# A hybrid decoder block on eight cores: from hand order to a list schedule, with the input projections by seven block products

## The chip, the cores and the metric

The kernel runs on the eight NeuronCores of one Trainium2 chip. Each core does one sequence of the batch; the cores share no data. The metric is the time of one execution in device microseconds, that of the slowest core. A core has five engines with their own in-order instruction queues: TensorE (PE, matmul, with its weight loads PEld), VectorE (DVE), ScalarE (ACT), GpSimd (POOL) and SyncE (SP). They wait for each other with semaphores. Matmuls write into banks of a memory called PSUM (`ps` in the traces), which ScalarE and VectorE read out. GLA is the gated linear attention of the code below.

Some executions fall into a slower state: the cores of one die, or of both, are granted a lower TensorE clock, and the run takes 2 to 16% longer.

## The reference, cut to what matters

```python
D_MODEL, BATCH, SEQ = 2048, 8, 2048      # one batch element a core
u = rmsnorm(h)
# one input projection, 12,816 columns wide, cut into ten parts
aq, ak, av, gq, gk, gv, g_lr, g_r, gate_a, gate_b = split(u @ w_in)
attn_o = swa_sink_attention(aq, ak, av, sinks)      # 32 heads, window 128, softmax with a sink
gate_logit = g_lr @ gla_gate_w2 + gla_gate_b        # rank 16
gla_o = gla(gq, gk, gv, log_sigmoid(gate_logit)/16) # 4 heads, chunks of a linear attention
gla_o = rmsnorm(gla_o) * silu(g_r)
h = h + (sigmoid(gate_a) * attn_o + sigmoid(gate_b) * gla_o) @ w_out
h = h + (silu(v2 @ w_gate) * (v2 @ w_up)) @ w_down  # v2 = rmsnorm(h), hidden 5632
out = rmsnorm(h)
```

The "mixer" below is everything from the input projection to the merged branches. The kernel treats the 2048 tokens in two halves of 1024.

## The kernel before: the parts that the change touches

The mixer's projections are plain matmuls, 16 steps of 128 along the contraction, with 512 moving columns:

```python
def proj_feat(c, units, col0, hf, m=128):
    b = nps()
    mm([(b[0:m, :], wu[units[k // 8]][:, k % 8, col0:col0 + m],
         xx[:, k, hf * 512:(hf + 1) * 512], k == 0, k == 15) for k in range(16)], ...)
```

The FFN's up projections already use seven block products in place of eight: a 2x2 block product after Strassen and Winograd, with sums of weights (`ws`) and of inputs (`xs`) made on VectorE beforehand, and partial products combined afterwards. Two column groups (`q`) alternate, so that a bank has two products' time, 3.5 us, to be read out.

The order is written by hand: generators that are woven together, and each engine runs its instructions in program order.

```python
prev = chain2(ov, a_chain(c, h, range(NT)))       # GLA chain, then attention of head h
weave(g_proj(c, h), prev, 32, 18)                 # ... woven into the projections of head h+1
```

In attention, the mask is a multiplication on VectorE, and the softmax sums are a matmul by ones over both key blocks, next to the value product:

```python
act(pt[:], banks[half][:, :], AF.Exp, scale=0.125)
vtt(p3, p3, amask[:, kb, :].unsqueeze(1).to_broadcast([128, 4, 128]), ALU.mult)
...
for b, kind in ((bd, 0), (bo, 1)):     # bd: sums by ones, bo: values; kb 1 and 0, both halves
    ... items.append((b[half * 64:half * 64 + 64, :], l_, e8["a_P%d" % (half * 2 + kb)][:], ...))
    mm(items)
```

The softmax here doesn't subtract the row's maximum and nothing guards it: scores larger than these inputs give would overflow.

## Time and profile before

| kernel before | |
|---|---|
| median of the first 3 runs | 3831.0 us (3831.0, 4110.6 in the slow state, 3801.0) |
| span of the profiled core | 3798.9 us |
| PE, DVE, ACT, POOL busy | 95%, 43%, 31%, 5% |
| mean granted clock | 0.981 |

The head of the profile page, with the busy time of each engine, and the two rows of the 40-slice timeline for PE and for its clock (each digit is tenths):

```profile
span 3798.9 us, 47609 instructions; the slowest of 8 cores (3779.1 to 3798.9 us)
PE 3593.0 (95%) x17296; PEld 1623.0 (43%) x17296; DVE 1633.8 (43%) x2661; ACT 1187.8 (31%) x2231; POOL 195.1 (5%) x354
PE   3899999998999999899889999999979999999997
PEclk9999999998999999999999999999999999999999
```

PE is busy nearly always, but "busy" hides things, because a recorded matmul lasts 0.38 us and the next one starts after 0.216 us. The price of a matmul is read from starts. The next fence has lines of three answers of the PE timeline (start, length, what, how many in a row):

```profile
138.20 1.04 PE L332 MATMUL ps<-wu_67,xnT_108 128*128 128x256 bf16 x8
139.08 1.04 PE L332 MATMUL ps<-wu_66,xnT_108 128*128 128x256 bf16 x8
...
143.63 1.89 PE L332 MATMUL ps<-wu_69,xnT_108 128*128 128x512 bf16 x8
145.36 1.89 PE L332 MATMUL ps<-wu_68,xnT_108 128*128 128x512 bf16 x8
...
606.03 1.89 PE L332 MATMUL ps<-wu_67,xnT_108 128*128 128x512 bf16 x8
607.85 0.61 PE L621 MATMUL ps<-a_q_110,kT_109 64*128 64x512 bf16 x4
608.39 1.90 PE L332 MATMUL ps<-wu_66,xnT_108 128*128 128x512 bf16 x8
```

Eight matmuls of 512 columns take 145.36 - 143.63 = 1.73 us, 0.216 us each. Eight of 256 take 0.88 us, 0.109 each. The last three lines show: the product that starts at 606.03 is through at 607.76, but the four half-array matmuls of attention (64 rows) start at 607.85; they need two times 0.216 us, until 608.28, and the next full product starts at 608.39. Going into the half-array form and out of it cost 0.09 and 0.11 us. Such a trip is called an excursion below.

PE's waits in the kernel before, from the view of waits (total us, times, longest):

```profile
PE ps L332 <- DVE xnT_108 L376: 31.9, 2, 16.7
PE ps L332 <- DVE hy_0_152 L365: 29.5, 2, 15.4
PE ps L332 <- ACT g_la L356: 25.2, 1, 25.2
PE ps L867 <- DVE fb_2_145 L365: 10.7, 1, 10.7
```

They are few and long: the start (`xnT`, `g_la`), and changes of stage (`hy`, `fb`).

### The profile page before, as it was taken

How to read it: one execution, taken by the hardware profiler on the slowest of the kernel's cores; microseconds unless marked ns; L12 is line 12 of the kernel's file. 1: busy time of each engine (PE TensorE's matmuls, PEld its weight loads, DVE VectorE, ACT ScalarE, POOL GpSimd, SP SyncE). 2: the span in 40 equal slices, each digit the busy share in tenths (PEclk: the TensorE clock that was granted, in tenths of full speed). 3: DMA queues.
4: the chain of work that ended last, by engine and by line, in shares of the span. 5: the costliest groups of instructions: out<-in, count | busy, mean ns of one | idle time of the engine just before them, and what ended most of it. 6: DMA issues, size and time to landing. Idle time of an engine off the chain costs nothing.

```text
span 3798.9 us, 47609 instructions; the slowest of 8 cores (3779.1 to 3798.9 us)
## 1 busy us (share of the span) xinstructions
PE 3593.0 (95%) x17296; PEld 1623.0 (43%) x17296; DVE 1633.8 (43%) x2661; ACT 1187.8 (31%) x2231; POOL 195.1 (5%) x354
## 2 busy tenths in 40 slices
PE   3899999998999999899889999999979999999997
PEld 1444444443444444344344444444434444444443
DVE  1224444444476621565212344444454775146623
ACT  1243535353333300222113444454533222012212
POOL 0000000000000000000000000000001000000000
PEclk9999999998999999999999999999999999999999
DMA  7344444444565688555973342425256687874474
GB/s 159 48 67 73 67 73 67 69 63 79 167 131 119 124 168 179 67 89 105 218 163 75 59 81 46 93 45 95 45 133 159 130 168 159 193 150 86 86 158 133
DMA packets 104504, 416.93 MB, mean 110 GB/s; under 512 B 12752, under 2 KB 13904, under 8 KB 69712
## 3 DMA queue, kind: packets, MB, share of 16 engines
q0 software_dynamic: 36432, 260.19, 40.7%
q1 hardware_dynamic: 67840, 153.68, 13.4%
q8 instruction: 141, 2.31, 0.3%
q14 instruction: 91, 0.75, 0.1%
HBM read 612.14 MB, written 60.82 MB: 177 GB/s over the span
## 4 chain that ended last, share of the span: by engine, by line
PE 87%; DMA 5%; DVE 4%; ACT 1%; issue 1%; SPq 0%; POOL 0%; DVEq 0%; ACTq 0%; POOLq 0%
PE ps L332 59%; PE ps L867 27%; DMA xts_225<-xT 1%; DMA px_230<-xT 1%; PE ps L340 1%; PE ps L621 1%; DMA wu_68<-wffn 1%; DMA h_0_99<-x 1%; DMA xts_226<-xT 1%; DVE xnT_108 L376 1%; DMA yd<-hy_6_158 1%; ACT g_Sb L356 0%; SPq L385 0%; DMA h1d<-hy_6_158 0%; DVE mT L370 0%
## 5 line engine op out<-in xcount | busy, mean ns | idle before, releaser
L356 ACT ACTIVATE g_Sb<-g_U,dec 128x512 bf16<-128x512 f32 x112 | 77.2, 722 | 151.6 <-DVE g_U L376 149.1
L370 DVE TENSOR_SCALAR mT<-ps,cols_sb 128x128 bf16<-128x128 bf16 x256 | 72.6, 283 | 107.1 <-PE ps L340 85.3
L332 PE MATMUL ps<-xnT_108,wu_66 128*128 128x512 bf16 x352 | 86.4, 390 | 31.9 <-DVE xnT_108 L376 31.9
L332 PE MATMUL ps<-wu_69,xnT_108 128*128 128x512 bf16 x384 | 90.8, 379 | 0.0
L332 PE MATMUL ps<-wu_70,xnT_162 128*128 128x512 bf16 x384 | 90.8, 379 | 0.0
L356 ACT ACTIVATE a_t_96<-a_t_96 128x512 f32<-128x512 f32 x64 | 40.4, 631 | 154.9 <-DVE a_t_96 L376 154.9
L332 PE MATMUL ps<-xnT_108,wu_67 128*128 128x512 bf16 x352 | 84.4, 383 | 1.2 <-DVE g_gn_85 L376 1.2
L867 PE MATMUL ps<-v2T_114,ws_0_141 128*128 128x512 bf16 x352 | 81.2, 385 | 3.2 <-DVE ws_0_141 L365 3.2
L867 PE MATMUL ps<-v2T_168,ws_0_195 128*128 128x512 bf16 x352 | 81.0, 384 | 3.2 <-DVE ws_0_195 L365 3.2
L332 PE MATMUL ps<-xnT_162,wu_68 128*128 128x512 bf16 x352 | 83.2, 379 | 0.0
L332 PE MATMUL ps<-xnT_162,wu_67 128*128 128x512 bf16 x352 | 83.2, 379 | 0.0
L400 POOL TENSOR_TENSOR st<-st,mhalf 128x1 f32<-128x1 f32 x80 | 47.9, 599 | 631.6 <-DVE st L372 631.6
L867 PE MATMUL ps<-v2T_114,ws_1_142 128*128 128x512 bf16 x352 | 79.6, 379 | 0.0
L867 PE MATMUL ps<-v2T_168,ws_1_196 128*128 128x512 bf16 x352 | 79.6, 379 | 0.0
L362 DVE CAST g_v<-ps 128x512 bf16<-128x512 f32 x32 | 22.1, 692 | 132.3 <-PE ps L332 131.4
L332 PE MATMUL ps<-xnT_108,wu_70 128*128 128x512 bf16 x320 | 76.6, 383 | 0.0
L332 PE MATMUL ps<-wu_68,xnT_108 128*128 128x512 bf16 x320 | 75.7, 379 | 0.0
L332 PE MATMUL ps<-wu_69,xnT_162 128*128 128x512 bf16 x320 | 75.7, 379 | 0.0
L332 PE MATMUL ps<-wu_70,xnT_108 128*128 128x512 bf16 x320 | 75.7, 379 | 0.0
L332 PE MATMUL ps<-wu_66,xnT_162 128*128 128x512 bf16 x320 | 75.7, 379 | 0.0
L332 PE MATMUL ps<-xnT_162,wu_69 128*128 128x512 bf16 x320 | 75.6, 379 | 0.0
L332 PE MATMUL ps<-xnT_108,wu_68 128*128 128x512 bf16 x320 | 75.6, 379 | 0.0
(1322 smaller groups left out, 7654.7 us busy)
## 6 DMA issues: line engine op xcount, KB each, us to landing
wu_67<-wmix POOLq DMA_DIRECT2D x24, 1024.0 KB, 13.5
wu_68<-wmix POOLq DMA_DIRECT2D x24, 1024.0 KB, 13.3
wu_66<-wmix POOLq DMA_DIRECT2D x23, 1024.0 KB, 12.3
wu_69<-wmix POOLq DMA_DIRECT2D x23, 1024.0 KB, 11.4
wu_70<-wmix POOLq DMA_DIRECT2D x22, 1024.0 KB, 13.2
wu_69<-wffn POOLq DMA_DIRECT2D x19, 1024.0 KB, 13.3
wu_70<-wffn POOLq DMA_DIRECT2D x19, 1024.0 KB, 13.5
wu_66<-wffn POOLq DMA_DIRECT2D x17, 1024.0 KB, 11.6
```

The lines of the kernel that those rows point to most:

```text
L332: r = e.matmul(o_, lhsT=l_, rhs=r_, start=s0, stop=s1)
L340: r = e.transpose(out=o_, in_=i_, identity=identb[:])
L356: S.op("act", lambda e: e.activation(out=o_, in_=i_, func=func, scale=scale, **kw), outs, ins)
L362: S.op("dve", lambda e: e.tensor_copy(out=o_, in_=i_), [o_], [i_])
L370: S.op("dve", lambda e: e.tensor_scalar(out=o_, in0=a, scalar1=s1, scalar2=None, op0=op0), [o_], ins)
L376: S.op("dve", lambda e: e.scalar_tensor_tensor(out=o_, in0=a, scalar=s, in1=b, op0=op0, op1=op1), [o_], ins)
L400: S.op("pool", lambda e: e.tensor_tensor(out=r, in0=a, in1=mhalf[:, 0:1], op=ALU.pow), [r], [a, mhalf[:, 0:1]])
L621: r = e.matmul(o_, lhsT=l_, rhs=r_, start=s0, stop=s1)
L867: r = e.matmul(bank[:, :], lhsT=w[:, k, :], rhs=x[:, k, :], start=first and k == 0, stop=k == 7, skip_group_check=True)
```

## The change

The kernel is written anew. Its intent, in four parts:

1. All mixer projections by seven block products too (k and v of the first half excepted): one matmul in eight goes away, and the partial products are combined on ScalarE and VectorE, now for one column group at a time.
2. The order is computed. Every operation gets a priority tag and a modelled cost. A list schedule then simulates all engines: on each engine it takes, of the operations that can start about earliest (within 0.08 us), the one with the lowest tag, and it gives temporaries their buffers and PSUM banks on the way. The result is a fixed order per engine, with the semaphore waits that it needs.
3. The masks move to GpSimd, and the softmax sums are added over the two key blocks on VectorE before the matmul by ones.
4. The gate logits, before an fp32 matmul, become one bf16 matmul over split operands.

Also, the first norm is done by token rows and transposed, and the output and down projections use pairs of 256-column matmuls. The core of the diff (cuts marked with `...`; most of the 1181 added lines are the same work in the new form):

```diff
+    LAT = 55.0
+    MARGIN = 80.0
...
+        def release(o):
+            t = 0.0
+            for p in o.preds:
+                lat = 0.0 if p.eng == o.eng and not p.dma and not o.dma and o.eng == "pe" else self.LAT
+                t = max(t, p.end + lat)
...
+            m = min(c[0] for c in cands) + self.MARGIN
+            for c in cands:
+                if c[0] <= m:
+                    return c
...
+    def groups(gs, order=(4, 2, 1, 5, 3, 7, 6), lead=12.0, cls="b"):
...
+                if m == 4:
+                    prod(True)
+                    z["m4"] = ftile("b")
+                    acopy(z["m4"][:], b[:, :], bonus=B)
+                elif m == 2:
+                    prod(True)
+                    vtt(z["m4"][:], b[:, :], z["m4"][:], ALU.add, bonus=B)
...
-            for half in range(2):
-                pt = e8["a_P%d" % (half * 2 + kb)]
-                act(pt[:], banks[half][:, :], AF.Exp, scale=0.125)
-                p3 = pt[:, :].rearrange("p (a b) -> p a b", a=4)
-                vtt(p3, p3, amask[:, kb, :].unsqueeze(1).to_broadcast([128, 4, 128]), ALU.mult)
...
+                    act(p[:], b[:, :], AF.Exp, scale=0.125)
+                    ...
+                    S.op("pool", lambda e, ...: e.affine_select(out=real(p3), in_=real(p3), pattern=pat, ...),
+                         [p3], [p3], cost=600.0)
...
+            mm(items, cost=125.0 * len(items))          # values
+            items = []
+            for half in range(2):
+                if len(kbs) == 2:
+                    vtt(P[(1, half)][:], P[(1, half)][:], P[(0, half)][:], ALU.add)
+                items.append((bd[half * 64:half * 64 + 64, :], onesb[:, :], P[(1, half)][:], True, True))
+            mm(items, cost=250.0)                       # sums
```

## The prediction

> **What bounds it now.** TensorE. The summary of engines shows PE busy 3593 of 3799 us (95%), DVE 43%, ACT 31%, POOL 5%; the chain of waits is 87% PE. The timeline gives the cost of one 128x128x512 bf16 matmul, start to start: eight in 1.73 us, 0.216 us each. That agrees with the Trainium skill, page "TensorE: Matmul & The Clock Gate", section "Wait — 56ns, not 53.3ns?" (215.7 ns warm). Two fp32 512-column matmuls take 0.86 us (two units each), eight 256-column ones 0.873 us (0.109 each), sixteen transposes with a new stationary operand each 0.895 us (0.056 each). Its section "Back-to-back issue gap" states about 81 ns sustained for 128 columns; this trace disagrees, and I use 0.056.
>
> Counting units of 0.216 us before, per half of the tokens: mixer projections 3200, output projection 512, FFN up 2464 (already seven products), FFN down 1408, attention 192, GLA 224, fp32 gate logits 32, transposes 32, low-rank 5; plus 64 once for the fp32 norm sums. Total about 16,200 units, 3500 us. The other 300 us of the span are idle PE (206 us: 58 at the start, 30 at the change of halves near 1805-1995, about 20 at each mixer's end and at the tail, 10 around FFN stages) and about 94 us of matmuls in stretches after such gaps, where the granted clock falls to 0.87-0.96 (windows by stage; mean 0.981).
>
> **What the change does.**
> - Mixer projections in seven products: -384 units in each half, -400 in the second (k, v too): -784.
> - Softmax sums: probabilities are added first on DVE: -64.
> - Gate logits as split bf16: -32, +8 for its selection matmul.
> - First norm by rows: -64 fp32, +32 transposes; next half's norm +32 transposes.
> - Smaller moving operands: output and down projections as 256-column pairs (+2 ns per pair, +8 us), token-major products as 128-column (+8 us).
> Sum: about -872 units, -188 us, +16 us: about 3326 us of dense PE.
>
> DVE and ACT get more. From the durations in the trace (PSUM combination 0.61 us start to start, copy 0.49, 128x2048 bf16 sum 1.13), a group of 12.1 us of PE needs about 6.3 us of DVE and 1.5-7.5 us of ACT. I estimate DVE 2050-2200 us (60%), ACT 45%. Both stay under PE, but a one-group order leaves one product (1.73 us) to evacuate a bank where the pair order left two, so small stalls appear; masks move to POOL (an estimate of 0.6 us each, the trace has none), whose memory port is shared with VectorE (skill, "GPSIMD Engine Reference", "Specifications").
>
> The list schedule fills gaps at stage changes, so I expect idle plus cold clock to fall from 300 to about 165 us: 50-60 at the start (8 MB of x must land), 20 at the tail, the rest scattered.
>
> All of the removed PE work is on the critical path. **Predicted: 3490 us (range 3410 to 3620), -9%.** Faster by over 2%: 0.94; within 2%: 0.04; slower: 0.02.
>
> **Right or wrong shows in:** PE busy about 3350-3420 us, PE share 96-97%; DVE near 60%; mean granted clock 0.985 or more; idle PE under 120 us; POOL rising to 10-15%; dense windows without dips at 900, 1850 and 2800 us.
>
> **What would make it wrong:** 128-column products costing 81 ns instead of 56 (+95 us); GpSimd masks slow enough to hold attention; the fixed order misjudging DMA (three weight buffers, 2 MB each 12.1 us, 13 us to land), so PE waits for weight sums in every group; ACT near 90% in the gate stage; or, for the better, gaps nearly vanishing (3420).

## More of the kernel before

In the middle of the mixer PE hardly waits. This is the windows view of two stretches of steady mixer (stretch, its length, then busy us of PE, PEld, DVE, ACT, POOL, the granted clock, DMA share and GB/s):

```profile
380.00:855.00 475.00, 472.06 (x2350) 208.17 (x2349) 202.43 (x408) 229.91 (x423) 24.64 (x46) 1.00 0.43 68
2090.00:2755.00 665.00, 659.44 (x3295) 293.96 (x3295) 273.29 (x564) 311.28 (x576) 36.53 (x68) 1.00 0.35 66
```

PE is at 99.3% and VectorE at 42% there.

## The result

| | kernel before | changed kernel |
|---|---|---|
| runs | 3831.0, 4110.6 (slow), 3801.0, 3800.3 | 3631.0, 3624.0, 3989.6 (slow), 3618.9 |
| median of all | 3816.0 us | 3627.5 us |
| ratio of fast runs | | 0.9525 (0.9478 to 0.9571) |

The output is correct. The ratio is the mean time of one kernel's fast runs over that of the other's fast runs of the same rounds, so it is not quite the ratio of the medians. The change saves 4.8%, and the median of all runs lies just above the predicted range (3410 to 3620). The predicted saving was almost twice the measured one.

The profile after, the same lines as before:

```profile
span 3629.4 us, 63127 instructions; the slowest of 8 cores (3590.9 to 3629.4 us)
PE 3429.4 (94%) x23256; PEld 2023.3 (56%) x23256; DVE 2182.4 (60%) x3628; ACT 1356.1 (37%) x2642; POOL 531.3 (15%) x901
PE   4999999999999999999999999999999999999998
PEclk9999999999999999999999999999999999999999
```

PE is busy 164 us less, but its share fell from 95% to 94%. The small matmuls cost what was assumed. This is the PE timeline inside a token-major projection (128 columns):

```profile
138.35 1.95 PE L567 MATMUL ps<-wsum,x_l 128*128 128x128 bf16 x32
140.13 1.95 PE L567 MATMUL ps<-wsum,x_s 128*128 128x128 bf16 x32
```

32 of them take 1.78 us, 0.056 us each, where the Trainium skill ("TensorE: Matmul & The Clock Gate", section "Back-to-back issue gap") gives about 81 ns sustained. The measurement decides; this risk of the prediction did not come true.

PE's waits look quite different now:

```profile
PE ps L575 <- DVE h L631: 57.6, 29, 22.5
PE ps L575 <- ACT h L597: 29.8, 38, 1.2
PE ps L567 <- DVE h L619: 21.1, 21, 1.9
PE ps L567 <- POOL h L978: 16.0, 23, 1.0
PE ps L567 <- ACT f L603: 11.6, 20, 1.1
PE ps L567 <- DVE f L619: 11.2, 11, 2.7
```

The first line is mostly the start and the norms between stages (22.5 us in one wait). The others are new: many waits, mostly of a microsecond or less, for the normalised GLA output (`h L597`), the softmax sums (`h L619`), the masks (`h L978`) and the read-out of partial products (`f`). They lie in the mixer, as the windows view of steady mixer stretches shows:

```profile
180.00:810.00 630.00, 591.01 (x3897) 292.25 (x3895) 475.55 (x810) 366.51 (x716) 149.11 (x243) 1.00 0.46 82
1980.00:2520.00 540.00, 513.45 (x3500) 258.05 (x3498) 417.19 (x707) 316.87 (x616) 132.70 (x212) 1.00 0.44 80
```

PE busy fell from 99% to 94-95% there, while VectorE went from 42% to 76 to 77%.

### A ledger of PE's time

Busy time hides what a gap costs, so I counted differently. Every matmul record was given its start-to-start price (columns / 2.4 + 2.5 ns; half of that for a half-array matmul, a quarter for a quarter-array one; the timelines above agree with it: 0.216, 0.109 and 0.056 us). An fp32 matmul counts twice, as the timeline of the kernel before shows, two in 0.86 us:

```profile
59.02 1.02 PE L332 MATMUL ps<-g_cum,onesf 128*128 128x512 f32 x2
59.88 1.02 PE L332 MATMUL ps<-g_eg,onesf 128*128 128x512 f32 x2
```

The sum is the dense work. What is left of the span is overhead, put to the stage in which it falls. The prices are an estimate worked out from the timelines; the rest is arithmetic on the trace. Each column is one core with complete records, rounded. The row of mode switches is the number of excursions (128, 203 and 206) times the mean extra time of those that no wait disturbs (0.21, 0.25 and 0.24 us); it is a part of the other rows.

| overhead, us | before | changed | run lat (below) |
|---|---|---|---|
| start, up to the low-rank projection | 85 | 55 | 61 |
| two mixers | 77 | 168 | 106 |
| (array mode switches, most of them in the mixers) | 27 | 51 | 50 |
| two output projections | 24 | 22 | 3 |
| first FFN and change of halves | 64 | 20 | 18 |
| second FFN and tail | 28 | 38 | 43 |
| all overhead | 278 | 304 | 231 |
| dense work | 3521 | 3325 | 3325 |
| span | 3798.9 | 3629.4 | 3555.8 |

The dense work fell by 196 us; the prediction said 172. The overhead, predicted to fall from 300 to 165 us, rose from 278 to 304. The gaps at the start shrank by 29 us, those around the first FFN by 44 and those at the output projections by 2; the mixers gave back 92, and the second FFN 10.

### The profile page after: what moved, and what is told of

It reads as the page before. It is cut to its first block, busy times and chain, and to the rows that moved or that the text cites. A ratio compares the mean times of both kernels' runs of the same rounds, so it can differ in the third digit from the quotient of the medians.

```text
span 3629.4 us, 63127 instructions; the slowest of 8 cores (3590.9 to 3629.4 us)
## 1 busy us (share of the span) xinstructions
PE 3429.4 (94%) x23256; PEld 2023.3 (56%) x23256; DVE 2182.4 (60%) x3628; ACT 1356.1 (37%) x2642; POOL 531.3 (15%) x901
## 4 chain that ended last, share of the span: by engine, by line
PE 67%; DVE 9%; DMA 8%; ACT 7%; issue 6%; POOL 1%; SPq 0%; DVEq 0%; ACTq 0%; POOLq 0%
PE ps L567 66%; ACT f L597 4%; DMA raw<-wffn 3%; DMA raw<-wmix 2%; DVE f L619 2%; ACT h L597 2%; DMA mr<-md 1%; DVE h L631 1%; DVE U L631 1%; PE ps L575 1%; DVE h L619 1%; DVE wsum L619 1%; DMA prow<-x 1%; POOL ssq L823 1%; ACT f L603 1%
## 5 line engine op out<-in xcount | busy, mean ns | idle before, releaser
L619 DVE TENSOR_TENSOR f<-ps,f 128x512 f32<-128x512 f32 x598 | 410.1, 686 | 587.8 <-PE ps L567 577.9
L603 ACT COPY f<-ps 128x512 f32<-128x512 f32 x558 | 324.4, 582 | 955.1 <-PE ps L567 954.1
L567 PE MATMUL ps<-x_s,raw 128*128 128x512 bf16 x2704 | 640.6, 380 | 8.3 <-DMA raw<-wffn 4.1
L567 PE MATMUL ps<-fw,ff 128*128 128x256 bf16 x5632 | 615.8, 273 | 0.0
L567 PEld LDWEIGHTS ps<-fw,ff 128*128 128x128 bf16 x5632 | 551.0, 98 | 65.6 <-issue 1.0
L619 DVE TENSOR_TENSOR wsum<-raw 128x1024 bf16<-128x1024 bf16 x558 | 380.9, 703 | 115.5 <-DMA raw<-wmix 62.5
L597 ACT ACTIVATE f<-f 128x512 f32<-128x512 f32 x544 | 338.6, 630 | 212.7 <-DVE f L631 75.6
L567 PE MATMUL ps<-x_l,raw 128*128 128x512 bf16 (+1 forms) x1416 | 331.4, 377 | 11.8 <-DVE f L619 11.2
L567 PE MATMUL ps<-x_h,raw 128*128 128x512 bf16 (+1 forms) x1416 | 327.9, 374 | 0.0
L567 PE MATMUL ps<-x_h,wsum 128*128 128x512 bf16 x1352 | 322.7, 382 | 2.5 <-ACT x_h L603 2.5
L619 DVE TENSOR_TENSOR f<-f,f 128x512 f32<-128x512 f32 x190 | 133.8, 704 | 243.5 <-ACT f L603 238.4
L597 ACT ACTIVATE h<-f 128x512 bf16<-128x512 f32 x240 | 151.1, 630 | 297.6 <-DVE f L619 292.7
L619 DVE TENSOR_TENSOR raw<-raw 128x1024 bf16<-128x1024 bf16 x372 | 257.4, 712 | 0.0
L978 POOL TENSOR_SCALAR_AFFINE_SELECT h<-h 128x512 bf16<-128x512 bf16 x248 | 180.1, 753 | 254.8 <-ACT h L597 254.3
```

Of the source, the lines that this page charges most:

```text
L567: r = e.matmul(real(o_), lhsT=real(l_), rhs=real(r_), start=s0, stop=s1, skip_group_check=True)
L597: return e.activation(out=real(o_), in_=real(i_), func=func, scale=scale if isinstance(scale, float) else real(scale), **kw)
L603: S.op("act", lambda e: e.copy(out=real(o_), in_=real(i_)), [o_], [i_], cost=0.835 * n + (50 if isps(i_) else 93), tag=tag, bonus=bonus)
L619: S.op(eng, lambda e: e.tensor_tensor(out=real(o_), in0=real(a), in1=real(b), op=op), [o_], [a, b], cost=cost, tag=tag, bonus=bonus)
L978: S.op("pool", lambda e, p3=p3, pat=pat, op=op, cm=cm: e.affine_select(out=real(p3), in_=real(p3), pattern=pat, compare_op=op, fill=0.0, b ...
```

## Experiments

All runs gave correct outputs. Ratios are to the kernel before in the same rounds. I compared three theories for the mixers' 168 us.

- **Theory A: the schedule's model is too quick.** The order is fixed, and it was computed with a delay of 0.055 us from the end of an operation to the start of its consumer elsewhere. The kernel can be matched to its trace operation by operation. Where the consumer's engine was free and waiting, it started later than the modelled end of the producer by these medians: PE to ACT 0.24 us, PE to DVE 0.32, ACT to PE 0.30, ACT to DVE 0.21, DVE to ACT 0.18, DVE to PE 0.23, POOL to ACT 0.18. So the order puts PE operations where their inputs do not exist yet, and PE, in order, waits.
- **Rival B: no room.** VectorE at 76% and ScalarE at 58% can't serve seven products in time, whatever the order.
- **Rival C: single suspects.** The half-array excursions (75 more than before, most of them since values and sums are now two operations), or GpSimd's masks.

One chain shows theory A at work. The changed kernel, all engines, around the end of a GLA block (lines left out):

```profile
210.57 0.20 ACT L597 ACTIVATION_READ_ACCUMULATOR junk<-ps 128x1 f32 x1
211.98 1.89 PE L567 MATMUL ps<-x_l,raw 128*128 128x512 bf16 x8
211.98 0.15 DVE L626 TENSOR_SCALAR ssq<-ssq 128x1 f32<-128x1 f32 x1
...
212.69 0.58 POOL L651 DMA_DIRECT2D raw<-wmix  x1 [3.81 <-PE ps L567]
...
213.29 0.57 POOL L823 TENSOR_TENSOR ssq<-ssq,mhalf 128x1 f32<-128x1 f32 x1
213.96 0.69 ACT L597 ACTIVATE h<-ps,ssq 128x512 bf16<-128x512 f32 x1 [0.30 <-POOL ssq L823]
...
214.79 0.38 PE L575 MATMUL ps<-identb,h 128*128 128x128 bf16 x4 [0.93 <-ACT h L597]
```

The root goes from VectorE to GpSimd, where it stands behind a weight load that itself waited for PE, then to ScalarE, then to PE's transposes. The scaling by ScalarE starts at 213.96, and the transposes 0.83 us later; the model has 0.53 us of cost and 0.055 of delay, 0.58. A difference of this kind comes on top at every hop, and PE stands still for 0.93 us. The records alone would not tell all of it: the Trainium skill ("Perfetto Trace Analysis", section "Tensor Engine Instruction (MATMUL, LD_WEIGHTS)") says that a matmul's recorded end is an estimate, and that the acknowledgement and the semaphore follow; here ACT started a median of 0.09 us after the recorded end of the PE operation that it waited for.

### Run lat: only the modelled delays

```diff
-                lat = 0.0 if p.eng == o.eng and not p.dma and not o.dma and o.eng == "pe" else self.LAT
+                lat = 0.0 if p.eng == o.eng and not p.dma and not o.dma and o.eng == "pe" else self.lat(p)
+    LATS = {"pe": 280.0, "act": 220.0, "dve": 220.0, "pool": 200.0, "sp": 55.0}   # DMA stays at 55
```

(The same delays count for the release of a buffer, and between two operations of one engine other than PE. The run does not tell these apart from the delays between engines.)

> Changed kernel with one thing altered: the list schedule's model of the delay from an instruction's end to its consumer on another engine, 0.055 us in the change, is set to 0.20-0.28 us by producer, near what the trace of the changed kernel shows (0.17 to 0.32). No work is added or removed; only order and buffer homes change. Theory A (the static order puts consumers where a too short delay says, so PE waits in the mixer): about 3555 us against 3625 for the changed kernel (3530 to 3585), PE gaps in the two mixer stages fall from about 95 to under 45 us. Rival B (VectorE at 70-80% and ScalarE at 60% in the mixer have too little room, whatever the order): within 15 us of 3625. Rival C (the loss is array mode switches, about 61 us): within 15 us as well, switches unchanged.

Measured: 3557.5, 3561.5 and 3558.3 us (and 3879.5 slow), ratio 0.9346 (0.9328 to 0.9365). The same operations in another order are 66 us faster than the changed kernel. Theory A's figure is met to within 5 us. PE's gaps in the mixers fell from 95 to 36 us (expected: under 45), while the excursions stayed (203 and 206). Rivals B and C, which expected nothing of this edit, fall as causes of these 66 us. PE's waits and the windows of steady mixer (core 6, whose records are complete):

```profile
PE ps L580 <- DVE h L636: 49.6, 16, 21.9
PE ps L572 <- DVE f L624: 15.5, 15, 2.4
...
PE ps L580 <- ACT h L602: 6.5, 7, 1.1
...
PE ps L572 <- DVE h L624: 4.1, 9, 0.7
```

```profile
180.00:780.00 600.00, 590.94 (x3908) 295.18 (x3908) 472.05 (x813) 360.46 (x717) 157.12 (x243) 1.00 0.47 86
1940.00:2500.00 560.00, 551.78 (x3720) 277.54 (x3718) 436.62 (x753) 337.57 (x671) 153.16 (x232) 1.00 0.48 87
```

The waits for the GLA output fell from 29.8 to 6.5 us, those for the softmax sums from 21.1 to 4.1. PE is at 98.5%, and VectorE is even a little fuller than before the edit, 78 to 79% against 76 to 77%: fullness by itself was not what held PE. The same chain in run lat:

```profile
214.18 1.89 PE L572 MATMUL ps<-x_l,raw 128*128 128x512 bf16 x8
214.22 0.14 DVE L631 TENSOR_SCALAR ssq<-ssq 128x1 f32<-128x1 f32 x1
...
214.89 0.58 POOL L656 DMA_DIRECT2D raw<-wmix  x1 [3.66 <-DVE ssq L631]
...
215.50 0.57 POOL L828 TENSOR_TENSOR ssq<-ssq,mhalf 128x1 f32<-128x1 f32 x1
215.91 1.89 PE L572 MATMUL ps<-x_s,raw 128*128 128x512 bf16 x8
216.17 0.69 ACT L602 ACTIVATE h<-ps,ssq 128x512 bf16<-128x512 f32 x1 [0.30 <-POOL ssq L828]
...
217.64 0.39 PE L580 MATMUL ps<-identb,h 128*128 128x128 bf16 x4
```

The chain takes just as long, from the root's sum to the scaling 1.95 us against 1.98. But here the order puts one more product (`x_s,raw`, 1.73 us) before the transposes, and PE does not wait at all.

### Runs u130 and u0: the dose

```diff
-    LAT = 55.0
+    LAT = 130.0      # u130;  0.0 in u0
```

> Changed kernel with the one delay constant at 0.13 us in place of 0.055 (dose between the change and run lat). Theory A, dose and effect: between the two, 3575 to 3595. If run lat was only a lucky order, no trend: 3560 or 3625 or anything else.

> Changed kernel with the delay constant of the schedule's model at zero in place of 0.055 us: the dose below the change. Theory A (too short a delay puts consumers too early): slower than the changed kernel by 15 to 45 us, 3640 to 3670. If the order of run lat was only lucky: anywhere, about 3600 to 3650 without a trend.

Measured: u130 3570.4 and 3564.0 us (three more runs were slow), ratio 0.9368 (0.9340 to 0.9396); u0 3656.7 to 3665.2 us in four fast runs, ratio 0.9616. With delays of 0, 0.055, 0.13 and 0.20 to 0.28 us the time goes 3660, 3625, 3567, 3559. (In these two runs the one constant also serves DMA, which stays at 0.055 in lat.) A lucky order would hardly follow the dose. u0 fell into its band. u130 missed its band and lies 8 us below it: 58 of the 66 us are there at 0.13. No delay longer than that of lat was run, so it is not shown that the measured delays are the best ones; what is shown is that 0.055 is too short.

### Runs classic and classic_lat: what the seven products are worth

The mixer's projections by eight products again, read straight from PSUM, without sums of weights or inputs; in classic_lat with the delays of run lat.

```diff
+    def groups_c(gs):                     # used for all mixer projections
+        for half in range(2):
+            for sub in range(2):
+                for (r, tok, use) in st:
+                    b = bank("b")
+                    for k in range(16):
+                        ms.append((b[:, :], r[:, k, sub * 128:(sub + 1) * 128],
+                                   XB[("l" if k < 8 else "h") + z][:, k % 8, :], k == 0, k == 15))
+                    mm(ms, ...); use(sub, half, b, None)
-        xsums(...)                        # of the mixer, both halves
```

> Changed kernel with the mixer projections (and k, v of the second half) by eight products again, read straight from PSUM; no weight sums and no input sums in the mixer. Dense PE work rises by 784 units of 0.216 us, 169 us. If that saving was wholly on the critical path and the waits have other causes (A): 3625 + 150 to 175, so about 3785, about 0.99 of the kernel before. Rival B (the seven products' VectorE and ScalarE load causes the mixer's waits): the waits go with that load, so no more than 3625 + 120 = 3745.

> Eight products in the mixer (as in run classic) and the longer delays in the schedule's model (as in run lat). The seven products were worth 108 us in the changed kernel (3733 against 3625) though they take 165 us of dense work out. If the missing 57 us are the short delays alone, the gap to lat (3560) widens to 150-165: 3710 to 3725. If they are the price of evacuating each partial product in any order (more consumers, one product of time each), the eight-product kernel gains from the delays about as much as the seven-product one: 3670 to 3695, worth 110 to 135 us.

Measured: classic 3729.5 to 3733.9 us in four fast runs, ratio 0.9801 (0.9784 to 0.9818); classic_lat 3694.4 and 3696.2 us. A third run of 3730.9 also counts as fast, though one die had a granted clock of only 0.981, so its ratio of 0.9736 has a wide interval (0.9648 to 0.9824); I use the other two. (The undisturbed die of the third run took 3681 to 3692 us, as in those two.)

By the ledger, eight products take 3490 us of dense work, 165 more than seven. In the changed kernel they cost 3733 - 3625 = 108 us more: rival B's bound of 3745 holds, theory A alone, which gave about 3785, does not, and 57 us of the saving were eaten. With better delays they cost 3695 - 3559 = 136 us more, at the edge of the lower of my two bands. The overhead in the mixers agrees in kind: seven products 168 us in the changed kernel and 106 in run lat, eight products 104 and 66. So load is a part of the story. Better delays win back 28 of the 57 us; the other 29 were not won back, and no run shows what holds them.

### Runs bdone and maskdve: two suspects by themselves

bdone puts the softmax sums back on PE, in one operation with the value product. maskdve puts both masks back on VectorE.

```diff
-            mm(items, cost=125.0 * len(items))
-            items = []
-            for half in range(2):
-                if len(kbs) == 2:
-                    vtt(P[(1, half)][:], P[(1, half)][:], P[(0, half)][:], ALU.add)
-                items.append((bd[...], onesb[:, :], P[(1, half)][:], True, True))
-            mm(items, cost=250.0)
+            for kb in kbs:
+                for half in range(2):
+                    items.append((bd[...], onesb[:, :], P[(kb, half)][:], kb == kbs[0], kb == kbs[-1]))
+            mm(items, cost=125.0 * len(items))
```

```diff
-                    S.op("pool", lambda e, ...: e.affine_select(...), [p3], [p3], cost=600.0)      # maskdve
+                    vtt(p3, p3, amask[:, kb, :].unsqueeze(1).to_broadcast([128, 4, 128]), ALU.mult)
```

> Changed kernel with the softmax sums back on PE, in one PE operation with the value product: +64 units (+14 us dense), one excursion into the half-array mode less in each of 64 attention blocks (about 0.19 us each, -12 us), and no wait of PE for the VectorE sums (24 us of gaps in the changed kernel). If those gaps and switches are what is lost (C): about 3603 us. Theory A: the gap of 24 us moves partly to other consumers, 3615 to 3640.

> Changed kernel with both masks back on VectorE (about 0.34 us each, four per attention block, plus one small one per GLA block that also saves a ScalarE copy). If GpSimd's masks are what holds PE (20 us of gaps name it): about 3600 us. Theory A and B: VectorE gets 90 us more in the mixer, the waits move, 3620 to 3650.

Measured: bdone 3623.6, 3629.3 and 3626.6 us, ratio 0.9527 (0.9504 to 0.9550); maskdve 3621.1, 3618.5 and 3612.6 us, ratio 0.9499 (0.9481 to 0.9518). bdone lies in theory A's band, maskdve between the two bands. Neither differs from the changed kernel (0.9478 to 0.9571) by more than the noise. The waits of PE in bdone, and then in maskdve, show why:

```profile
PE ps L575 <- ACT h L597: 31.7, 39, 1.5
PE ps L567 <- POOL h L978: 27.2, 30, 1.9
PE ps L567 <- ACT f L603: 20.9, 31, 1.4
```

```profile
PE ps L568 <- DVE h L620: 32.8, 47, 3.1
PE ps L576 <- ACT h L598: 26.9, 33, 1.2
PE ps L568 <- ACT f L604: 22.0, 30, 2.8
```

In bdone the 21 us for the sums are gone and the excursions fall from 203 to 132 (by the ledger's estimate from 51 to 30 us), but waits for the masks rise from 16 to 27 and those for ScalarE's read-outs from 12 to 21. The mixers' overhead falls by only 12 us in all, and the sums' matmuls add 13 us of dense work. In maskdve the waits for GpSimd are gone and those for VectorE's `h` take their place. So a wait that the profile names need not be worth its time: here, taking one hop away moved much of the wait to the next.

### Run tagorder: the choice by time switched off

```diff
-    MARGIN = 80.0
+    MARGIN = 1000000000.0
```

> Changed kernel with the list schedule's choice by time switched off: each engine takes the placeable operation of lowest priority tag, whenever it would start (the window of 0.08 us is made endless). Same work. If choosing by modelled time is what fills gaps: 40 to 90 us slower than the changed kernel, 3665 to 3715. If the choice by time does nothing useful with these wrong delays: within 15 us of 3625.

Measured: 3708.4 and 3716.9 us (two more runs slow). That is about 88 us slower than the changed kernel. So even with wrong delays the choice by time gains much; the longer delays of run lat add 66 us to that.

### Runs lat_sw_bdone and lat_sw: the model made truer still

Both add to run lat 0.2 us for an excursion into the half-array form, and GpSimd times nearer to the trace. lat_sw_bdone also moves the softmax sums to PE as bdone did.

```diff
-            mm(items, cost=125.0 * len(items))
+            mm(items, cost=108.0 * len(items) + 200.0)
-            mm(items, cost=250.0)
+            mm(items, cost=416.0)
-                    mm([(b[:, :], kk, aq[ps, :, n * 128:(n + 1) * 128], True, True)])
+                    mm([(b[:, :], kk, aq[ps, :, ...], True, True)], cost=208.0 if half == 0 else 108.0)
-  cost=600.0, 480.0, 250.0     # GpSimd: large mask, root, small mask
+  cost=640.0, 560.0, 300.0
```

> Run lat, with the array mode switches (about 0.2 us per half-array operation) and measured GpSimd times in the schedule's model, and with the softmax sums on PE in one operation with the value product (as in bdone). About 95 mode switches fewer (0.16 us each, -15 us), +14 us dense, and VectorE has 43 us less: 3540 to 3560, so at or a little under lat.

> As lat_sw_bdone but with the softmax sums left on VectorE: tells the schedule's mode-switch and GpSimd costs apart from the moved sums. If the moved sums do nothing (as in bdone beside the changed kernel): 3545 to 3560, the same as lat_sw_bdone (3554). If fewer mode switches are what made it faster than lat: 3560 to 3570.

Measured: lat_sw_bdone 3544.6, 3555.6, 3552.7 and 3556.0 us, ratio 0.9329 (0.9306 to 0.9352); lat_sw 3545.7 and 3549.5 us, ratio 0.9317 (0.9290 to 0.9344), with four of its six runs slow (its profile too; what is read from it here is core 5, on the undisturbed die). Both are a little faster than run lat, and their intervals overlap with each other and with that of lat, so the order among the three is not settled. Between these two, too, the moved sums make no difference that shows. Any of the three beats both kernels, by 6.5 to 6.8% over the kernel before.

## Why the prediction was wrong, point by point

- **What bounds the kernel: right.** PE, with 0.216, 0.109 and 0.056 us by column count.
- **The work left: right; the work removed: mis-sized.** Dense PE work in the changed kernel: 3326 us predicted, 3325 counted; PE busy 3429 us, a little over 3350 to 3420. But 196 us went, not 172. The prediction says that an fp32 matmul takes two units, and then counts the 128 of them at one, both in the total before (3500 us, counted 3521) and in what is removed. The slip cancels in the predicted time. DVE 60% and POOL 15% as said; ACT 37%, not 45%. Granted clock 0.991 to 0.995 as said.
- **The step that failed: "I expect idle plus cold clock to fall from 300 to about 165 us".** It measured 304, more than the 278 of the kernel before. Idle PE was 200 us, not under 120. The start (55 us) and the tail (14 us) came as predicted; it was "the rest scattered" that was mis-sized: 235 us where some 90 were left for it, 168 of them in the mixers. The prediction took it that a list schedule closes gaps, and did not ask whether its model of the delays is true. The code had the modelled delay of 0.055 us in plain view, and the trace of before shows that they are longer (matmuls recorded at 0.38 us and started every 0.216); I did not hold one against the other. Run lat gives back 66 of the 137 us by which the time exceeded the point prediction; of the other 71 us the cause is open.
- **A part of that step: the "about 94 us of matmuls in stretches after such gaps, where the granted clock falls".** That was a misreading. In the kernel before only about 30 us of overhead stand in stretches of lower clock outside of waits; some 27 us are mode switches, and some 21 us were no overhead at all, but the fp32 matmuls that the count took at half. This list schedule did not fill the switches, and the change adds 75 excursions. That a switch costs time, the Trainium skill says ("TensorEngine Tiling (Array Packing)", section "Key Properties": changing the tiling mode drains TensorE). The trace agrees, with 0.09 us going in and 0.11 us coming out; the prediction should have counted them. In bdone, 71 excursions fewer, against 13 us more of matmuls, saved no time.
- **"All of the removed PE work is on the critical path": too strong.** Of 165 us of dense work that the seven products save, 108 us came through, 136 us with better delays.
- **"A one-group order leaves one product (1.73 us) to evacuate a bank ... so small stalls appear": right in kind, not sized.** PE's waits for read-outs (`f` of ScalarE and VectorE) are 23 us in the changed kernel.
- **No dips at 900, 1850 and 2800 us: partly right.** The change of halves went from 64 us of overhead with the first FFN to 20; the output projections still had 22, and lost nearly all of it in run lat.

What stays open: 205 to 231 us of overhead in the three best runs. About 60 us are the start, 42 to 52 us are mode switches by the ledger's estimate, and I have not tried to remove either. How much the choices besides the delay (the window, the tags, the bank limits) still cost was not tested, and the split gate logits were not undone by themselves.

## What to carry to other kernels

A computed order depends on the delays in its model: before trusting it, match operations to trace records and measure the time from producer to consumer for each pair of engines, waiting included, not just the cost of each operation. When many small waits of different names appear on the bounding engine, take one away and see whether the sum falls; if it moves to the next name, no single engine is to blame, and the order itself is to be tested. Count the bounding engine's work by start-to-start price and keep a ledger of the rest, because busy shares hide both the gaps and the drains. Price every kind of matmul from the timeline: here the fp32 matmuls at half their price would have hidden that the overhead rose.

## What the Trainium skill lacked or had wrong

- "TensorE: Matmul & The Clock Gate", "Back-to-back issue gap": about 81 ns sustained for 128 columns and 131 for 512. The runs show 56 ns (32 matmuls in 1.78 us, each with new weights) and 216 ns (8 in 1.73 us). Its section "Wait — 56ns, not 53.3ns?" is right.
- The same page ("Seeing it yourself") states a 13/16 clock once three cores of a die run dense matmuls, held while the load lasts. In the fast profiles of the kernel before, the changed kernel and lat, all eight cores ran dense mixer and FFN stretches, and the clock records hold shares of 1.00 and 0.50 alone. The state itself is seen in the one slow profile (lat_sw): 238 to 381 us at 0.8125 on each core of the slow die, none on the other.
- "TensorEngine Tiling (Array Packing)", "Key Properties", has the drain at a mode switch but no figure: 0.09 us going into a half-array form and 0.11 us coming out of it.
- No page that I read has the time from a producer to a waiting consumer by pair of engines: 0.18 to 0.32 us after the producer's modelled end.
- "GPSIMD Engine Reference" has no price for a mask by affine select: for 128x512 bf16 a median of 0.635 us, up to 1.157 us, with VectorE 76% busy beside it. The page's statement of a shared port with VectorE ("Specifications") fits the spread, but no run here isolates it.
